# A hybrid decoder layer on one core: stores and parameter loads issued by GpSimd, the sampled tokens' loads by ScalarE

## The chip, the cores and the metric

The kernel runs on one core of one Trainium2 chip. The metric is the time of one execution on the device, in microseconds (us). Five engines work on the core: TensorE (PE in the profile; its weight loads are the row PEld), VectorE (DVE), ScalarE (ACT), GpSimd (POOL) and SyncE (SP). SP computes nothing; it issues transfers. A transfer (DMA) is issued by an instruction in the queue of SP, ACT or POOL, and an instruction that has to wait holds up everything behind it in the same queue.

## The reference

One layer with two token mixers and an MLP, in float32. It runs over a prompt of 2048 tokens and over a second batch of 8 x 4 sampled tokens that continue from given states; both use the same weights. Cut to what matters:

```python
xn = rms_norm(x, norm_mix_pre)
qk, v_m, o_m, gates, q_a, k_a, v_a = split(xn @ w_in)      # 1024 -> 2312 columns
qk, conv_new = short_conv(qk, conv_buf, conv_w)            # causal, 4 taps, silu
state_new, h = mlstm_chunk(state, (q, k, v, ig, lf))       # 4 heads, chunks of 128, state 64 x 128 per head
att = swa(q_a, k_a, v_a, sinks)                            # 8 heads, window 128, ALiBi, sinks
mix = concat(mlstm_output(h, o_m), rms_norm(att)) @ w_out
x = x + rms_norm(mix)
f = square(relu(rms_norm(x) @ w_up)) @ w_down              # 1024 -> 4096 -> 1024
x = x + rms_norm(f)
x = x + sigmoid(x @ w_pgate) * (p @ w_pproj)
```

It returns the new x of both batches and the new states: for each batch the mLSTM matrix C, its vector n and scalar m, the last three rows of the convolution's input, and the window's keys and values. For the sampled tokens C is 8 x 4 x 64 x 128.

## The kernel before

**Precision by pairs.** A matmul in float32 is done as three matmuls of a faster type: each operand is split into a high part, cast by ACT (L248 for weights, L227 for activations), and the rest, subtracted by DVE or POOL (L249, L228). For weights the helper is `wsplit` (L247), and `weng` (L242) gives the subtraction to POOL and DVE in turn.

**The ring of weights.** `Ring` (L251) holds 5 raw buffers and 7 pair buffers. A weight is asked for in the order of a plan written out by hand (L383). `get` (L270) loads it raw, splits it and, if the plan needs the same weight again, `keep` (L266) stores the finished pair, 512 KB, to DRAM; every later use reloads that pair (L274) instead of splitting again. A store in `keep` has to wait for the subtraction of its pair; a reload has to wait until TensorE has finished with the buffer that it overwrites. There are 242 such stores and 698 reloads.

**Stages.** First the projection by w_in over six chunks of the prompt, with attention (`swa_chunk`) and mLSTM (`mlstm_chunk`) running between its matmuls; their outputs go to DRAM as `yd` (L915, L1041). The sampled tokens' projection goes to DRAM as `zsd` (L591). Then three groups of blocks, each with w_out (`mix_mm`, `post_mix`, which stores x1 at L1429), sixteen steps of the MLP (`mlp`), and the gate (`gate_mm`, whose `finish` stores the output at L1765). From the fifth step of the first group (third of the later ones) the up matmuls use a product scheme with seven products for eight, whose weight sums are formed by `product` (L284), on POOL for the most part. A step of that kind splits and stores 7 pairs of w_up and 4 of w_down in the first group; the later groups reload nearly all.

**The sampled tokens.** In the first group's first steps `decode_mlstm` and `decode_swa` (L1070, L1256) run between the MLP's matmuls. They load states, caches and `zsd`; L1211 and L1212 load the mLSTM state into the tile `scs` in sixteen transfers, L1253 and L1254 store it in sixteen, half of them 128 KB and half 1 KB. The 1 KB ones (the vector n) write single numbers that lie apart in SBUF.

**Order.** TensorE's order is the program's, written out by the class `Flow`, which advances side work by estimated due times. The instructions of the other engines and queues are put in order at build time by a planner that takes what it reckons to be ready first. So the order of two instructions in a queue need not be the program's, and it is fixed when the kernel runs.

**Who issues.** All transfers of the program are issued by SP, with the exception of six small ones by ACT (L847). In the code, the name `dma` stands for SP's issue:

```python
    dma = nc.sync.dma_start
```

Of the kernel before, what the change touches and what calls it, by code (L numbers as in the profile page):

```python
# [24 lines left out]
DT = 4  # L25
# [170 lines left out]
def hybrid_layer(ctx: ExitStack, tc: tile.TileContext, A, O):  # L196
# [4 lines left out]
    dma = nc.sync.dma_start  # L201
# [49 lines left out]
    class Ring:  # L251
# [227 lines left out]
    def parameters():  # L479
        dma(prow[0:8], A["norm_ffn_pre"].rearrange("l (k p) -> (l k) p", p=P))  # L480
        dma(prow[8:12], A["mlstm_norm"].rearrange("l (k p) -> (l k) p", p=P))
        for s in range(2):
            dma(prow[12:16, s * AD : (s + 1) * AD], A["attn_norm"][:, s * 256 : (s + 1) * 256].rearrange("l (j d) -> (l j) d", d=AD))
        dma(prow[16:32], A["conv_w"].rearrange("l j (k p) -> (l j k) p", p=P))
        dma(bi[:, 0:1], A["b_gates"][:, 0:MH].rearrange("l h -> h l"))
        dma(bi[:, 1:2], A["b_gates"][:, MH : 2 * MH].rearrange("l h -> h l"))
        dma(sink, A["attn_sinks"][0:1, :].broadcast_to((P, AH)))
# [405 lines left out]
    def mlstm_chunk(r, blocks):  # L893
# [16 lines left out]
        def finish():  # L910
            if todo and len(r.get("o", ())) == len(blocks):
# [3 lines left out]
                dma(yd[blocks[i]][0], y)  # L915
# [64 lines left out]
    def swa_chunk(r, blocks):  # L980
# [45 lines left out]
        def values(i, j):  # L1026
# [14 lines left out]
            dma(yd[b][1], y)  # L1041
# [28 lines left out]
    def decode_mlstm(sp):  # L1070
        cb = sp.tile([P, NCB], F32, name="cb")
        dma(cb, A["const_b"][:, 0:NCB])
# [6 lines left out]
        dma(zqk, zsd[:, Z_QK : Z_QK + 512])  # L1079
        zg = sp.tile([NS, 2 * MH], F32, name="zg")  # L1080
        dma(zg, zsd[:, Z_G : Z_G + 2 * MH])


        for b in range(DB):
            dma(O[11][0, b], zsd[b * DT + 1 : b * DT + 4, Z_QK : Z_QK + 512])
        for out, cache, off in ((12, "cache_swa_k", Z_KA), (13, "cache_swa_v", Z_VA)):
# [3 lines left out]
            dma(oc[:, WIN - DT : WIN, :], zsd[:, off : off + 128].rearrange("(b t) c -> b t c", t=DT))  # L1090
# [87 lines left out]
        dma(va[:, :, 0:128], zsd[:, Z_V : Z_V + 512].rearrange("p (h v) -> p h v", h=MH))  # L1178
# [46 lines left out]
        dma(so, zsd[:, Z_O : Z_O + 512])  # L1225
# [4 lines left out]
        dma(yds[0], y)  # L1230
# [699 lines left out]
```

## Time and profile before

| | |
|---|---|
| Time, median of 3 runs | 2704.3 us (2697.03 to 2705.15) |
| The profiled execution | 2707.11 us, span 2705.3 us |
| TensorE's mean granted clock | 0.973 of full speed |
| Busy share of the span | PE 95%, PEld 82%, DVE 53%, ACT 36%, POOL 15% |
| Transfers | 626.95 MB, nearly all through SP's queue (q1) |
| HBM | 470.22 MB read, 155.25 MB written |

The span runs from the first instruction to the last of one execution. Busy shares do not count the issuing of transfers, so SP has none, and a queue that waits looks idle. In a row of the timeline the brackets say how long the engine stood still before the instruction and what ended that wait. In the chain of waits each piece is the work that the next piece waited for.

### The profile page before, as it was taken

How to read it: one execution, taken by the hardware profiler on the slowest of the kernel's cores; microseconds unless marked ns; L12 is line 12 of the kernel's file. 1: busy time of each engine (PE TensorE's matmuls, PEld its weight loads, DVE VectorE, ACT ScalarE, POOL GpSimd, SP SyncE). 2: the span in 40 equal slices, each digit the busy share in tenths (PEclk: the TensorE clock that was granted, in tenths of full speed). 3: DMA queues.
4: the chain of work that ended last, by engine and by line, in shares of the span. 5: the costliest groups of instructions: out<-in, count | busy, mean ns of one | idle time of the engine just before them, and what ended most of it. 6: DMA issues, size and time to landing. Idle time of an engine off the chain costs nothing.

```text
span 2705.3 us, 38958 instructions
## 1 busy us (share of the span) xinstructions
PE 2562.3 (95%) x14282; PEld 2227.0 (82%) x14282; DVE 1439.4 (53%) x3109; ACT 980.7 (36%) x2163; POOL 410.6 (15%) x517
## 2 busy tenths in 40 slices
PE   6899999999896899999999999999999998999998
PEld 5787888788675789888877888899988877999986
DVE  3675756655553275555573474444446345444453
ACT  3554454444443344433451352122223133222231
POOL 1310110100210134444440112000001010000010
PEclk8999999999898999999999999999999998999999
DMA  6766656567877547776688965555556885777786
GB/s 210 278 239 203 207 187 207 196 235 238 219 268 156 167 153 275 261 254 237 226 284 311 328 222 185 187 194 188 189 184 234 297 303 192 257 257 259 255 297 231
DMA packets 233728, 626.95 MB, mean 232 GB/s; under 512 B 37067, under 2 KB 76063, under 8 KB 233522
## 3 DMA queue, kind: packets, MB, share of 16 engines
q1 hardware_dynamic: 233490, 624.44, 68.0%
q8 instruction: 113, 1.85, 0.3%
q14 instruction: 77, 0.63, 0.1%
q10 hardware_dynamic: 48, 0.03, 0.0%
HBM read 470.22 MB, written 155.25 MB: 231 GB/s over the span
## 4 chain that ended last, share of the span: by engine, by line
PE 78%; DMA 8%; DVE 8%; ACT 2%; POOL 2%; issue 2%; SPq 1%; POOLq 0%; ACTq 0%; DVEq 0%
PE up L145 23%; PE dn L145 21%; PE mo L145 5%; PE pg L145 5%; PE v L145 3%; PE o L145 3%; DMA w<-wk 2%; PE gv L145 2%; PE qa L145 2%; PE pv L145 1%; PE aT L149 1%; PE aO L145 1%; PE qk L145 1%; DMA out_dram<-scs 1%; PE aS L145 1%
## 5 line engine op out<-in xcount | busy, mean ns | idle before, releaser
L145 PE MATMUL dn<-w,hh 128*128 128x512 f32 x1792 | 567.8, 398 | 15.4 <-DMA w<-wk 9.6
L145 PEld LDWEIGHTS dn<-w,hh 128*128 128x128 f32 x1792 | 334.3, 189 | 95.1 <-issue 11.3
L1683 DVE TENSOR_TENSOR f<-f,dn 128x512 f32<-128x512 f32 x420 | 287.7, 686 | 227.3 <-PE dn L145 226.5
L145 PE MATMUL dn<-w,hl 128*128 128x512 f32 x896 | 354.3, 395 | 0.0
L1647 DVE TENSOR_TENSOR re<-up,re 128x384 f32<-128x384 f32 (+1 forms) x280 | 144.3, 515 | 311.6 <-PE up L145 307.4
L145 PEld LDWEIGHTS dn<-w,hl 128*128 128x128 f32 x896 | 169.3, 189 | 39.4
L1648 ACT COPY re<-up 128x384 f32<-128x384 f32 (+1 forms) x40 | 17.9, 448 | 381.4 <-PE up L145 381.4
L249 POOL TENSOR_TENSOR w<-wr,w 128x512 fp32r<-128x512 f32 (+1 forms) x76 | 105.4, 1389 | 303.2 <-ACT w L248 199.7
L1573 ACT ACTIVATE re<-re 128x384 f32<-128x384 f32 (+1 forms) x160 | 78.8, 493 | 175.1 <-DVE re L1647 173.0
L248 ACT CAST w<-wr 128x512 fp32r<-128x512 f32 (+1 forms) x152 | 93.4, 619 | 132.0 <-DMA wr<-in_w_up_dram 29.5
L228 DVE TENSOR_TENSOR hl<-re,hh 128x384 fp32r<-128x384 f32 (+1 forms) x192 | 118.8, 619 | 38.1 <-ACT hh L227 37.6
L248 ACT CAST w<-wb 128x512 fp32r<-128x512 f32 x98 | 60.4, 621 | 199.7 <-PE dn L145 134.4
L145 PE MATMUL up<-ut00h,w 128*128 128x384 f32 x320 | 88.7, 348 | 24.7 <-ACT w L248 23.5
L249 DVE TENSOR_TENSOR w<-wr,w 128x512 fp32r<-128x512 f32 (+1 forms) x76 | 59.0, 778 | 83.1 <-ACT w L248 81.1
L249 POOL TENSOR_TENSOR w<-wb,w 128x512 fp32r<-128x512 f32 x70 | 93.8, 1359 | 54.1 <-ACT w L248 54.1
L1574 ACT ACTIVATE re<-re 128x384 f32<-128x384 f32 (+1 forms) x192 | 94.8, 494 | 5.9
L227 ACT CAST hh<-re 128x384 fp32r<-128x384 f32 (+1 forms) x192 | 92.5, 482 | 6.8
L1002 DVE CUSTOM_DVE_ANT_0 s<-aS,cst,sink 128x256 f32<-128x256 f32 (+1 forms) x128 | 56.9, 472 | 71.5 <-PE aS L145 71.2
L145 PE MATMUL up<-ut01h,w 128*128 128x384 f32 x320 | 88.9, 340 | 0.0
L1008 ACT ACTIVATE s<-s,swt 128x257 f32<-128x257 f32 (+1 forms) x128 | 63.4, 497 | 69.8 <-DVE swt L1005 69.0
L1394 POOL TENSOR_TENSOR f<-f,gffn 128x512 f32<-128x512 f32 x16 | 21.4, 1352 | 416.9 <-ACT j L1392 416.6
L145 PEld LDWEIGHTS up<-ut00h,w 128*128 128x128 f32 x320 | 60.2, 194 | 27.1 <-ACT w L248 24.3
(1468 smaller groups left out, 6305.4 us busy)
## 6 DMA issues: line engine op xcount, KB each, us to landing
w<-wk SPq DMA_DIRECT2D x678, 512.0 KB
wk<-w SPq DMA_DIRECT2D x238, 512.0 KB
wr<-in_w_down_dram SPq DMA_DIRECT2D x64, 256.0 KB
wb<-in_w_up_dram SPq DMA_DIRECT2D x28, 512.0 KB
w<-wk SPq DMA_DIRECT2D x20, 528.0 KB
x<-in_x_prompt_dram SPq DMA_DIRECT2D x16, 512.0 KB
y<-yd SPq DMA_DIRECT2D x32, 256.0 KB
xr<-in_x_prompt_dram SPq DMA_DIRECT2D x16, 512.0 KB
```

The costliest lines, as they stand in the source:

```text
L145: ins = self.pe.matmul(out, lhsT, rhs, start=start, stop=stop)
L149: self.issue(self.pe.transpose(out, src, ident), out, src, 2)
L227: act.copy(hi, src)
L228: dve.tensor_tensor(lo, src, hi.bitcast(F32), ALU.subtract)
L248: act.copy(hi, src)
L249: (eng or weng()).tensor_tensor(lo, src, hi.bitcast(F32), ALU.subtract)
L1002: dve.tensor_tensor_reduce(s_[:, s, lo : 2 * P], pS[:, s, lo:], bias[:, j, lo:], 1.0 if s == 0 else 0.0625, sink[:, h : h + 1], ALU.add, A ...
L1008: act.activation(e_, e_, AF.Exp, bias=nm[:, s : s + 1], accum_out=sm[:, s : s + 1])
L1573: act.activation(t, src, AF.Relu)
L1574: act.square(t, t)
L1647: add = lambda out, a, b: dve.tensor_tensor(out, a, b, ALU.add)
L1683: dve.tensor_tensor(out(i), out(i), ps[i], ALU.add)
```

## The change

Two further names are added. `put` issues on POOL's queue, `fetch_small` on ACT's. All stores except the two big copies from DRAM to DRAM (L1089) become `put`, and with them the eight loads of parameters; the loads in `decode_mlstm` and `decode_swa` become `fetch_small`. SP keeps the loads of x, weights, kept pairs, gains, y, Wt and p. Nothing else changes: the same transfers with the same shapes.

```diff
-    dma = nc.sync.dma_start
+    dma, put, fetch_small = nc.sync.dma_start, nc.gpsimd.dma_start, nc.scalar.dma_start
...
         def keep(self, key, t):
             self.kept[key] = dram.tile(list(t.shape), U32, name=f"{self.nm}k{len(self.kept)}")
-            dma(self.kept[key], t.bitcast(U32))
+            put(self.kept[key], t.bitcast(U32))
...
     def parameters():
-        dma(prow[0:8], A["norm_ffn_pre"].rearrange("l (k p) -> (l k) p", p=P))
+        put(prow[0:8], A["norm_ffn_pre"].rearrange("l (k p) -> (l k) p", p=P))
...
-        dma(zsd[:, zoff : zoff + n], t[:, :n])
+        put(zsd[:, zoff : zoff + n], t[:, :n])
...
-                dma(yd[blocks[i]][0], y)
+                put(yd[blocks[i]][0], y)
...
-                dma(cs[er, :, h, 0:128], c_in[e, h])
-                dma(cs[er, :, h, 128], n_in[e, h])
+                fetch_small(cs[er, :, h, 0:128], c_in[e, h])
+                fetch_small(cs[er, :, h, 128], n_in[e, h])
...
-                dma(c_out[e, h], cs[er, :, h, 0:128])
-                dma(n_out[e, h], cs[er, :, h, 128])
+                put(c_out[e, h], cs[er, :, h, 0:128])
+                put(n_out[e, h], cs[er, :, h, 128])
...
-        dma(bias_s, A["const_b"][:, NCB : NCB + nk])
+        fetch_small(bias_s, A["const_b"][:, NCB : NCB + nk])
...
-        dma(x1dst, f[b][:n])
+        put(x1dst, f[b][:n])
...
-        dma(O[2].rearrange("l b (p e) d v -> e d (l b p) v", e=2)[e], C[er, :, 0:128])
-        dma(O[3].rearrange("l b (p e) d -> e d (l b p)", e=2)[e], C[er, :, 128])
+        put(O[2].rearrange("l b (p e) d v -> e d (l b p) v", e=2)[e], C[er, :, 0:128])
+        put(O[3].rearrange("l b (p e) d -> e d (l b p)", e=2)[e], C[er, :, 128])
...
-        dma(dst, o[:n])
+        put(dst, o[:n])
```

## Rows read from the trace of the kernel before

**Rows 1.** The page, part 1: busy us (share of the span) and instructions.
```profile
PE 2562.3 (95%) x14282; PEld 2227.0 (82%) x14282; DVE 1439.4 (53%) x3109; ACT 980.7 (36%) x2163; POOL 410.6 (15%) x517
```
**Rows 2.** Windows: length, then busy us and count per engine, clock, DMA share, GB/s.
```profile
core 0: us, PE busy (x) PEld busy (x) DVE busy (x) ACT busy (x) POOL busy (x), PEclk, DMA share, GB/s
0.00:60.00 60.00, 36.74 (x171) 31.27 (x171) 23.84 (x46) 22.57 (x38) 10.96 (x23) 0.85 0.66 195
...
700.00:735.00 35.00, 26.33 (x96) 19.46 (x96) 21.52 (x37) 14.08 (x27) 5.17 (x5) 0.79 0.91 183
...
800.00:867.00 67.00, 57.77 (x307) 46.88 (x306) 34.17 (x90) 28.66 (x63) 7.37 (x8) 0.90 0.75 197
867.00:890.00 23.00, 1.76 (x7) 0.92 (x6) 0.84 (x1) 1.28 (x3) 1.27 (x1) 0.60 0.92 102
...
1038.00:1351.00 313.00, 313.00 (x1559) 281.42 (x1558) 177.38 (x270) 130.31 (x241) 144.08 (x109) 1.00 0.68 249
```
**Rows 3.** TensorE's timeline: start, us, instruction, in brackets its idle time before.
```profile
17.55 0.39 PE L145 MATMUL gv<-w,x0h 128*128 128x264 f32 x1 [2.40 <-ACT w L248]
...
22.21 1.11 PE L149 MATMUL x10t<-ident,x 128*128 128x128 f32 x4 [2.60 <-DVE x L584]
...
60.97 0.69 PE L145 MATMUL qa<-x0h,w 128*128 128x384 f32 x1 [4.87 <-ACT w L248]
...
733.58 1.22 PE L145 MATMUL mo<-w,yt00h 128*128 128x512 f32 x2 [5.34 <-DVE f L1488]
...
888.43 0.69 PE L145 MATMUL up<-ut00h,w 128*128 128x384 f32 x1 [20.85 <-ACT w L248]
```
**Rows 4.** SP's queue: what it waited for, us in total, times, longest.
```profile
SPq L268 <- POOL w L249: 363.0, 132, 11.0
...
SPq L268 <- DVE w L249: 99.0, 76, 7.6
```
**Rows 5.** The chain that ended last, 840 to 890: start, us, what.
```profile
856.73 20.28 DMA out_dram<-scs
...
877.66 0.60 SPq L359
...
878.31 10.17 DMA wr<-in_w_up_dram
```
**Rows 6.** POOL's timeline, at the start and from 845 to 890.
```profile
5.95 0.57 POOL L499 TENSOR_TENSOR x0t<-x0t,nhalf 128x1 f32<-128x1 f32 x1 [4.82 <-DVE x0t L498]
...
850.51 1.28 POOL L249 TENSOR_TENSOR w<-wr,w 128x512 fp32r<-128x512 f32 x1 [4.49 <-ACT w L248]
888.51 1.27 POOL L249 TENSOR_TENSOR w<-wr,w 128x512 fp32r<-128x512 f32 x1 [36.72 <-DMA wr<-in_w_up_dram]
```
**Rows 7.** The chain that ended last, 700 to 735.
```profile
706.58 9.32 DMA out_dram<-C
...
715.91 13.77 DMA wr<-in_w_out_dram
```
**Rows 8.** SP's timeline at the start: start, us, instructions that follow one another.
```profile
9.82 2.05 SPq L268 DMA_DIRECT2D wk<-w  x3
...
12.96 1.78 SPq L456 DMA_DIRECT2D x<-in_x_prompt_dram  x2
```
**Rows 9.** Issues by line, ns min/median/max, first and last start; L268 from 1038 to 1351.
```profile
L268 SPq DMA_DIRECT2D wk<-w x110: 319/320/929, 1039.7 to 1349.2; - x110
...
L847 ACTq DMA_DIRECT2D mbd<-Mt x6: 246/246/514, 57.4 to 617.1; - x6
...
L1211 SPq DMA_DIRECT2D scs<-in_state_mlstm_c_dram x8: 602/615/705, 820.7 to 835.3; - x8
```
**Rows 10.** TensorE's waits for reloaded pairs: us in total, times, longest.
```profile
PE dn L145 <- DMA w<-wk: 9.6, 3, 4.8
...
PE mo L145 <- DMA w<-wk: 7.3, 3, 3.8
```
**Rows 11.** SP's timeline at the end.
```profile
2702.64 0.33 SPq L1765 DMA_DIRECT2D out_dram<-ots  x1
```

More of the change, by code (lines that the diff above doesn't have):

```diff
@@ L479, in parameters @@
     def parameters():
-        dma(prow[0:8], A["norm_ffn_pre"].rearrange("l (k p) -> (l k) p", p=P))
-        dma(prow[8:12], A["mlstm_norm"].rearrange("l (k p) -> (l k) p", p=P))
+        put(prow[0:8], A["norm_ffn_pre"].rearrange("l (k p) -> (l k) p", p=P))
+        put(prow[8:12], A["mlstm_norm"].rearrange("l (k p) -> (l k) p", p=P))
         for s in range(2):
[L483 to L487, printed above, removed]
+            put(prow[12:16, s * AD : (s + 1) * AD], A["attn_norm"][:, s * 256 : (s + 1) * 256].rearrange("l (j d) -> (l j) d", d=AD))
+        put(prow[16:32], A["conv_w"].rearrange("l j (k p) -> (l j k) p", p=P))
+        put(bi[:, 0:1], A["b_gates"][:, 0:MH].rearrange("l h -> h l"))
+        put(bi[:, 1:2], A["b_gates"][:, MH : 2 * MH].rearrange("l h -> h l"))
+        put(sink, A["attn_sinks"][0:1, :].broadcast_to((P, AH)))
         yield 5.0
@@ L1040, in values @@
             act.copy(y.rearrange("p (j q) -> p j q", j=4), pO)
-            dma(yd[b][1], y)
+            put(yd[b][1], y)
             sq = sw.tile([P, 512], F32, tag="ya", name=f"sq{b}")
@@ L1071, in decode_mlstm @@
         cb = sp.tile([P, NCB], F32, name="cb")
-        dma(cb, A["const_b"][:, 0:NCB])
+        fetch_small(cb, A["const_b"][:, 0:NCB])
         mask_s = cb[:, 0:32]
@@ L1078, in decode_mlstm @@
         zqk = sp.tile([NS, 512], F32, name="zqk")
-        dma(zqk, zsd[:, Z_QK : Z_QK + 512])
+        fetch_small(zqk, zsd[:, Z_QK : Z_QK + 512])
         zg = sp.tile([NS, 2 * MH], F32, name="zg")
-        dma(zg, zsd[:, Z_G : Z_G + 2 * MH])
+        fetch_small(zg, zsd[:, Z_G : Z_G + 2 * MH])
         for b in range(DB):
-            dma(O[11][0, b], zsd[b * DT + 1 : b * DT + 4, Z_QK : Z_QK + 512])
+            put(O[11][0, b], zsd[b * DT + 1 : b * DT + 4, Z_QK : Z_QK + 512])
         for out, cache, off in ((12, "cache_swa_k", Z_KA), (13, "cache_swa_v", Z_VA)):
@@ L1224, in decode_mlstm @@
         so = sp.tile([NS, 512], F32, name="sso")
-        dma(so, zsd[:, Z_O : Z_O + 512])
+        fetch_small(so, zsd[:, Z_O : Z_O + 512])
         act.activation(so, so, AF.Tanh, scale=0.5)
@@ L1229, in decode_mlstm @@
         mlstm_finish(num, col[:, 8:12], so, y, NS, "dm")
-        dma(yds[0], y)
+        put(yds[0], y)
         for h in range(MH):
@@ L1266, in decode_swa @@
         vc = sp.tile([WIN, DB, 128], F32, name="svc")
-        dma(kc, A["cache_swa_k"].rearrange("l b s k d -> s (l b) (k d)"))
-        dma(vc, A["cache_swa_v"].rearrange("l b s k d -> s (l b) (k d)"))
+        fetch_small(kc, A["cache_swa_k"].rearrange("l b s k d -> s (l b) (k d)"))
+        fetch_small(vc, A["cache_swa_v"].rearrange("l b s k d -> s (l b) (k d)"))
         snk = sp.tile([P, 2], F32, name="ssnk")
@@ L1271, in decode_swa @@
         for g in range(4):
-            dma(snk[g * NS : (g + 1) * NS], sv[:, :, g].broadcast_to((NS, 2)))
+            fetch_small(snk[g * NS : (g + 1) * NS], sv[:, :, g].broadcast_to((NS, 2)))
         yield 15.0
@@ L1338, in decode_swa @@
         dve.tensor_scalar(y, y, rs[:NS], None, ALU.mult)
-        dma(yds[1], y)
+        put(yds[1], y)
     def decode():
@@ L1351, in hybrid_layer @@
     for o, c0 in ((6, 8), (7, 136)):
-        dma(O[o].rearrange("l b s k d -> (l b s) (k d)"), prev["va"][:, c0 : c0 + 128])
+        put(O[o].rearrange("l b s k d -> (l b s) (k d)"), prev["va"][:, c0 : c0 + 128])
     es_proj.close()
@@ L1532, in hybrid_layer @@
     dve.tensor_copy(cvo, pcv[:3, :])
-    dma(O[5].rearrange("l b j c -> (l b j) c"), cvo)
+    put(O[5].rearrange("l b j c -> (l b j) c"), cvo)
     es1.close()
```

16 lines of the change are left out of this document (8 added, 8 removed).

## The prediction

> **What bounds the kernel now.** Read the page's busy line first: TensorE's matmuls are busy 2562.3 of 2705.3 us [rows 1], so whatever the change does to other engines can only shorten the 143 us in which TensorE stands still, or lengthen them. The table by stage says where those lie [rows 2]: 23.3 us of 60 at the start (60 less 36.74), 8.7 of 35 between the projection and the first MLP, 21.2 of 23 in 867 to 890, and none of 313 in the ten steps from 1038 to 1351. Then TensorE's own timeline, for what ended each pause [rows 3]: one pause of 20.85 us waits for ACT's cast of a raw row of w_up; the others are of 2 to 5 us. Last the queue that issues the transfers: SP spent 363.0 us waiting for GpSimd's residual and 99.0 us for DVE's, both times only to be able to store a weight pair (L268) [rows 4]. In most of that time TensorE had work, so those sums are not the gain; what matters is what stood behind such a store in a stage where TensorE was dry.
>
> **The moved stores, one place at a time.** 377 issues leave SP for POOL: 242 weight pairs, 34 of y, 32 of yd, 17 of x1, 16 of the sampled state and 36 small ones. Their bytes stay the same; what changes is who stands behind them.
>
> *867 to 890.* The chain there is a store of scs that lands after 20.28 us, then at 877.66 the issue of the load of w_up (L359), which lands 10.17 us later [rows 5]. The split of the pair that it feeds starts on POOL at 888.51; the one before it ran at 850.51 and was over at 851.8 [rows 6]. From then on a raw buffer was free, so without the sixteen stores of scs ahead of it the load could go some 25 us earlier, at about 853, while TensorE first needs it at 867.6 (888.43 less 20.85). That leaves 14 us for a load that took 10.2 among the stores, plus cast 0.6 and split 1.3. But the same sixteen stores now stand in POOL's queue, and the odd split is POOL's: it may wait behind them. Bounds: nothing gained, or all 20.85. I take 16, nearer the upper end, because the data of the last store is there at 858 and only its slow landing holds the others.
>
> Against this stands a rule of the Trainium skill (DMA: Bandwidth & Descriptors, "Issuing engines are not separate DMA queues"): transfers issued by SP, ACT and GpSimd run on the same 16 engines and interleave, so another issuer saves issue time only. The row agrees that engines and not only the queue are short there: 0.92 busy at 102 GB/s [rows 2]. By the rule the early load would still share those engines with the stores; I make that a rival below.
>
> *700 to 735.* The same picture, smaller: two stores of C land after 9.32 us, a load of w_out behind them after 13.77 [rows 7], and TensorE pauses 5.34 at 733.58 [rows 3]. I take 4 (0 to 5.3).
>
> *Start.* SP issues three pair stores at 9.82, each waiting for its split, and only then at 12.96 the loads of x1 and x2 [rows 8]. TensorE pauses 2.40, 2.60 and 4.87 in the first 61 us behind such loads [rows 3]; I take 5 of these 9.9. Against it the eight parameter loads come to POOL, which at 5.95 must compute the first rstd (L499) [rows 6]; if they go ahead of it they cost 2 us at 0.25 each, the issue price on ACT [rows 9], or up to 5. I take 2. Net 3 gained.
>
> *Later loads.* Waits of TensorE for reloaded pairs sum to 9.6 (dn) and 7.3 (mo) [rows 10]. Most end when a buffer of the ring comes free, which the change does not touch, so I take 3 of 16.9 (0 to 10).
>
> **What POOL pays.** No row shows a DMA issued by POOL, so its price must be bounded. From below: 0.25 us, the issue on ACT, or 0.32, the same store on SP [rows 9]. From above there is no row, so I ask what POOL can bear. In the ten steps 1038 to 1351 it is busy 144.1 of 313 us and 110 pair stores fall there: (313 - 144.1) / 110 = 1.54 us of free time for each [rows 2, 9]. Up to that, less some for waits, the stores hide in POOL's idle time, and TensorE, at 100% there, does not feel them. I take 0.3 to 1.2 as likely, nearest to the SP row, and cost the steps at nothing; if that cover is gone each 0.1 us above 1.54 costs 12 x 11 x 0.1 = 13 us over the twelve steps. In between, a store in POOL's queue waits for DVE or ACT with POOL's next work behind it: sink copies (L998), the powers (L1406, L887), half of the pair splits. On SP these waits were 99 us for DVE's splits alone [rows 4]. Nearly all lie where TensorE is fed ahead; I take 3 us lost (0 to 10).
>
> The Trainium skill prices a GpSimd issue higher (DMA: Bandwidth & Descriptors, "Specifications"): about 1 us to the first byte against 0.6 for SP and ACT, descriptors being written by GpSimd itself. An estimate from that page: 14.4 + 11 x 1.0 = 25.4 us of POOL per step of 31.3, which still fits. No run here shows it yet.
>
> **What ACT pays.** 32 loads of the sampled tokens come to ACT between 735 and 895: at 0.25 us, ACT's row, 8 us; at 0.615, SP's row for the sixteen loads of scs, 20 us [rows 9]. ACT is busy 28.7 of 67 us there [rows 2], so over half falls in gaps, but relu and casts queue behind each block. I take 4 lost (0 to 10). SP loses the same issues; that is already in the 16 above.
>
> **End.** The last store goes out at 2702.64, after DVE's last operation, and the span ends at 2705.3 [rows 11]; issued by POOL it may land later by the unknown issue price: 1 lost (0 to 2).
>
> **Sum:** -16 - 4 - 3 - 3 + 3 + 4 + 1 = -18. The profiled execution took 2707.1 us (span 2705.3), 2.8 above the median of 2704.3; so 2707.1 - 18 = 2689 on its scale, and **2686** on the median's.
>
> **Rivals.**
> *POOL becomes the bound (slower).* If a pair store holds POOL for more than 1.54 us in the twelve steps, TensorE runs dry there. At 1.9 us that is 12 x 11 x 0.36 = 48 lost: 2686 + 48 = 2734. For it: POOL's splits share their stretch with DVE's, and waits for DVE come on top. Against: ACT's and SP's issues are 0.25 to 0.6. Chance 0.20. The Trainium skill (SBUF — State Buffer, "Who interferes with whom") speaks for this one: a DMA issued by GpSimd waits for its descriptors while some DVE modes hold a shared port; no row here shows such a wait.
> *The engines, not the queue (no change).* The early loads of 867 to 890 and 700 to 735 crawl beside the slow stores, so 16 becomes 4 and 4 becomes 0: -18 + 16 = -2, 2702. For it: engines 0.92 busy there. Against: the load had the stores ahead of it in its own queue when it took 10.17 us. Chance 0.20.
> *The stall changes its owner.* The split on POOL waits behind the sixteen stores until about 888, and ACT's 32 issues cost 10 instead of 4: -18 + 16 + 6 = +4, 2708. Chance 0.12; that the move is in the program's text but the order on the engines ends up the same is within it.
> *My forecast* keeps 0.48, with its own range 2666 to 2700.
>
> **Chances.** A measurement of this kernel can tell about 0.3%, 8 us. Faster: 0.48 of the forecast less a little, plus the better part of the second rival: 0.52. Within: 0.25. Slower: 0.23, the first rival and the end of the third. The range reaches from 2660 (the upper bounds of 700 to 735, the start and the late loads all met) to 2738 (the first rival).
>
> **What would show it.** The pause of 20.85 before an up matmul near 888 shrinks to about 5 and L359's load is issued near 853; x1's load is issued by 8 us; POOL's rows in the steps stay under 31 us with the issues counted, and TensorE stays at 100% there. It is wrong if TensorE pauses for POOL L249 in the steps (first rival), if the same pause stays and ends on DMA wr<-in_w_up_dram (second) or on POOL L249 (third), or if pauses appear behind ACT's issues.

## The result and the profile after

The changed kernel takes 2687.6 us (median of 5 runs, 2683.6 to 2687.7), the kernel before 2700.5 (5 runs, 2697.0 to 2705.2): ratio 0.9945, 95% interval 0.9931 to 0.996. The forecast was 2686. The profiled execution took 2687.7 us, with a span of 2685.6 against 2705.3 [rows 1]. So the two traces differ by 19.7 us, the medians by 12.9: the profiled execution of the kernel before was 6.6 us over its median. What follows accounts for the 19.7.

First the busy line of the page (engine, busy us, share, instructions):

```profile
PE 2546.3 (95%) x14282; PEld 2216.1 (83%) x14282; DVE 1473.3 (55%) x3109; ACT 981.4 (37%) x2163; POOL 613.3 (23%) x894
```

GpSimd's row now counts its 377 issues as instructions (894, and 517 before) and as busy time.

TensorE's idle time is 2685.6 - 2546.3 = 139.3 us, and was 2705.3 - 2562.3 = 143.0: only 3.7 us less. The other 16.0 us are TensorE's busy time itself, for the same instructions. The mean granted clock rose from 0.973 to 0.980: (1 - 0.973) x 2705.3 / 0.5 = about 146 us at the lower of its two levels (1.2 GHz) before, (1 - 0.980) x 2685.6 / 0.5 = about 107 us after. So the sum of idle time says little here, and neither do equal windows of time. To see where the time went, cut both traces at the same matmul (TensorE runs the same matmuls in the same order in both). The windows of the changed kernel so cut (columns: stretch and length, then as in [rows 2]: busy us and instructions of PE, PEld, DVE, ACT and POOL, granted clock, busy share of the DMA engines, GB/s):

```profile
0.00:51.20 51.20, 31.93 (x178) 29.80 (x179) 20.07 (x30) 20.31 (x36) 23.28 (x45) 0.93 0.90 278
51.20:98.90 47.70, 36.81 (x191) 33.28 (x189) 41.73 (x95) 25.89 (x60) 22.97 (x33) 0.86 0.80 273
...
691.10:748.90 57.80, 53.49 (x229) 41.34 (x230) 36.31 (x67) 26.04 (x50) 20.65 (x29) 0.93 0.91 276
748.90:805.40 56.50, 36.49 (x166) 29.87 (x164) 26.16 (x66) 18.83 (x40) 15.33 (x18) 0.82 0.70 232
805.40:874.60 69.20, 60.32 (x329) 50.62 (x328) 27.51 (x74) 24.19 (x53) 22.71 (x33) 0.93 0.77 162
...
1000.70:1365.50 364.80, 356.83 (x1758) 316.63 (x1757) 225.82 (x308) 151.17 (x279) 228.33 (x249) 1.00 0.64 244
...
2170.20:2280.10 109.90, 99.85 (x562) 85.25 (x561) 61.18 (x120) 43.79 (x96) 15.28 (x23) 0.95 0.74 266
```

Beside them the same work in the kernel before, from the same view of its trace (us):

```
work from .. to (before)   length before -> after   change   idle before -> after   clock
0 .. 63.1                    63.1 ->  51.2          -11.9       24.2 -> 19.3        0.84 -> 0.93
63.1 .. 101.7                38.5 ->  47.8           +9.3        2.9 -> 10.9        0.96 -> 0.86
101.7 .. 141.9               40.2 ->  34.6           -5.6        4.1 ->  1.2        0.92 -> 1.00
141.9 .. 641.3              499.5 -> 496.3           -3.2       19.2 -> 17.9        1.00 -> 1.00
641.3 .. 700.3               58.9 ->  61.2           +2.3        4.0 ->  6.5        0.95 -> 0.92
700.3 .. 770.2               70.0 ->  57.8          -12.2       11.3 ->  4.3        0.85 -> 0.93
770.2 .. 808.5               38.3 ->  56.5          +18.2        3.4 -> 20.0        0.96 -> 0.82
808.5 .. 901.3               92.8 ->  69.3          -23.5       30.5 ->  8.9        0.83 -> 0.93
901.3 .. 1021.6             120.2 -> 126.1           +5.9        1.4 ->  5.8        1.00 -> 0.99
1021.6 .. 1375.5 (steps)    354.0 -> 364.7          +10.7        0.0 ->  8.0        1.00 -> 1.00
1375.5 .. 2180.8            805.3 -> 804.7           -0.6       14.4 -> 12.0        0.99 -> 0.99
2180.8 .. 2300.8            120.0 -> 109.9          -10.1       15.8 -> 10.1        0.90 -> 0.95
2300.8 .. 2705.3            404.5 -> 405.5           +1.0       11.9 -> 14.6        0.99 -> 0.99
```

The net of -19.7 is 67 us gained less 47 given back. The 9.3 given back at 63.1 to 101.7 is a pause of 10.72 us (second line of the next block). DVE's recorded order now has L903, which stands until the transfer Wt<-mbd has landed (issued 65.48, 7.63 us), ahead of the tile s that TensorE waits for, and TensorE comes there 14 us earlier (63.91 for 78.18). No run takes it apart. TensorE's timeline names what ended the pauses that remain (start, length, [idle before <- releaser]); these answer to [rows 3]:

```profile
14.36 1.11 PE L149 MATMUL x00t<-ident,x 128*128 128x128 f32 x4 [14.36 <-DVE x1t L498]
...
74.63 0.66 PE L149 MATMUL aT<-ident,s 128*128 128x128 f32 x2 [10.72 <-DVE s L1012]
...
769.99 1.22 PE L145 MATMUL mo<-w,yt01h 128*128 128x512 f32 x2 [13.40 <-DMA w<-wk]
...
787.38 1.22 PE L145 MATMUL mo<-w,yt01h 128*128 128x512 f32 x2 [6.60 <-ACT f L1486]
...
854.87 0.69 PE L145 MATMUL up<-ut00h,w 128*128 128x384 f32 x1 [5.02 <-ACT f L1681]
...
879.93 0.69 PE L145 MATMUL up<-ut01h,w 128*128 128x384 f32 x1 [4.83 <-ACT re L1573]
...
1137.56 0.73 PE L145 MATMUL dn<-w,hh 128*128 128x512 f32 x2 [1.74 <-DVE f L1683]
```

The pause of 20.85 us is gone; three of 3 to 5 us stand in its place, one of them (862.88, 3.39 us, POOL w L249) not shown. They are at other matmuls: the one that waited 20.85 us now waits for nothing (858.87). New are 13.40 and 6.60 in the output projection, and ten waits of up to 1.7 us (8.0 in all) for DVE's sum L1683 in the steps.

**770 to 808.** The waits of SP's queue, then of ACT, between 735 and 800 (us in total, times, longest):

```profile
SPq L274 <- DMA scs<-in_state_mlstm_n_dram: 26.9, 3, 23.3
```
```profile
ACT sso L1226 <- DMA w<-wk: 17.0, 1, 17.0
```

(The second row names a transfer on the same semaphore; what L1226 reads is so, whose load ACT issued at 767.45.)

SP, whose queue now has only loads, stood 23.3 us (742.0 to 765.3) ahead of a reload of a weight pair until a load of scs had landed that ACT issued. The reload neither reads nor writes scs. In the record of this stretch SP's queue stands 23.31 us at a wait for two semaphores that ACT's transfers update. The transfers of SP and ACT take turns on the same eight, and one that is to use a semaphore first waits for the transfer that had it last. GpSimd's transfers there use eight others. Two queues so become one where the program's order interleaves them.

**The steps.** DVE's groups with the first line of the step's work, and GpSimd's store (count | busy us, mean ns | idle before), from the windows 1010 to 1375:

```profile
L1683 DVE TENSOR_TENSOR f<-f,dn 128x512 f32<-128x512 f32 x136 | 91.5, 684 | 65.6 <-PE dn L145 65.6
...
L249 DVE TENSOR_TENSOR w<-wr,w 128x512 fp32r<-128x512 f32 x23 | 30.4, 1324 | 1.8
...
L249 DVE TENSOR_TENSOR w<-wb,w 128x512 fp32r<-128x512 f32 x20 | 26.6, 1331 | 0.9
...
L268 POOL DMA_DIRECT2D wk<-w x121 | 66.7, 552 | 20.4 <-DVE w L249 10.9 <-POOL w L249 7.7 <-DVE re L1647 1.3
```

A store holds GpSimd 0.55 us, but DVE's splits take 1.32 us where they took 0.71 and 0.68 before. Not all of them do: in the steps as cut above 24 of 43 take 0.69, and 18, some two a step, 1.98 to 2.47. One of these, with GpSimd beside it (start, length):

```profile
1054.80 1.10 POOL L268 DMA_DIRECT2D wk<-w  x2
...
1055.73 2.04 DVE L249 TENSOR_TENSOR w<-wr,w 128x512 fp32r<-128x512 f32 x1
...
1055.92 1.30 POOL L249 TENSOR_TENSOR w<-wr,w 128x512 fp32r<-128x512 f32 x1
```

DVE's split starts during GpSimd's issue, GpSimd's own split follows the issue at once, and DVE's ends 0.55 us after GpSimd's. Where DVE's split starts as little ahead of an instruction of GpSimd with no issue running, it keeps its 0.69, and GpSimd's is the longer one (1.70 for 1.30):

```profile
1289.37 0.69 DVE L249 TENSOR_TENSOR w<-wb,w 128x512 fp32r<-128x512 f32 x1
1289.52 1.70 POOL L298 TENSOR_TENSOR wb<-wb,wb 128x512 f32<-128x512 f32 x1 [2.22 <-DMA wb<-in_w_up_dram]
```

Eight splits in this trace started during an issue with nothing of GpSimd right behind; they took 0.69 too. After a long split the sums L1683 come late, and TensorE waits for them.

### The profile page after: what moved, and what is told of

It reads as the page before. It is cut to its first block, busy times and chain, and to the rows that moved or that the text cites. A ratio compares the mean times of both kernels' runs of the same rounds, so it can differ in the third digit from the quotient of the medians.

```text
span 2685.6 us, 39181 instructions
## 1 busy us (share of the span) xinstructions
PE 2546.3 (95%) x14282; PEld 2216.1 (83%) x14282; DVE 1473.3 (55%) x3109; ACT 981.4 (37%) x2163; POOL 613.3 (23%) x894
## 4 chain that ended last, share of the span: by engine, by line
PE 72%; DMA 9%; DVE 8%; issue 4%; POOL 3%; ACT 3%; ACTq 0%; SPq 0%; POOLq 0%; DVEq 0%
PE up L145 19%; PE dn L145 19%; PE pg L145 6%; PE mo L145 4%; PE v L145 3%; PE o L145 2%; PE qk L145 2%; DMA wk<-w 2%; PE gv L145 2%; POOL w L249 2%; PE pv L145 1%; PE aT L149 1%; PE aO L145 1%; DMA w<-wk 1%; PE qa L145 1%
## 5 line engine op out<-in xcount | busy, mean ns | idle before, releaser
L1683 DVE TENSOR_TENSOR f<-f,dn 128x512 f32<-128x512 f32 x420 | 285.7, 686 | 218.0 <-PE dn L145 217.7
L268 POOL DMA_DIRECT2D wk<-w x242 | 134.1, 555 | 145.6 <-DVE w L249 109.6
L249 POOL TENSOR_TENSOR w<-wr,w 128x512 fp32r<-128x512 f32 (+1 forms) x76 | 102.0, 1342 | 81.8 <-ACT w L248 62.8
L249 POOL TENSOR_TENSOR w<-wb,w 128x512 fp32r<-128x512 f32 x70 | 89.9, 1295 | 100.8 <-ACT w L248 100.3
L249 DVE TENSOR_TENSOR w<-wr,w 128x512 fp32r<-128x512 f32 (+1 forms) x76 | 80.5, 1061 | 44.4 <-ACT w L248 42.4
```

The costliest lines, as they stand in the source:

```text
L249: (eng or weng()).tensor_tensor(lo, src, hi.bitcast(F32), ALU.subtract)
L268: put(self.kept[key], t.bitcast(U32))
L1683: dve.tensor_tensor(out(i), out(i), ps[i], ALU.add)
```

## The experiments

Each ratio is of 4 to 12 runs against 11 to 23 of the kernel before on the same chip. The change of each stretch against the kernel before, cut at the same matmuls, from the profiled execution of each (us):

```
                    0   142   641   700   770   808   901  steps  1376  2181  2301
                 -142  -641  -700  -770  -808  -901 -1022        -2181 -2301  -end    sum
changed          -8.2  -3.2  +2.3 -12.2 +18.2 -23.5  +5.9  +10.7  -0.6 -10.1  +1.0  -19.7
e1_small_on_sync -10.3 -4.2  +2.3 -10.1  -5.5 -21.1  +4.8  +10.9  -4.5 -10.5  -0.2  -48.4
e2_pairs_on_sync -7.2  -1.4   0.0  -7.9 +18.2  -6.6  +0.1    0.0  -3.6 -10.8  -2.6  -21.8
e3_only_pairs   -14.7  -0.9 +10.4 -10.7  -5.6  -2.7  +0.4  +14.9  -2.8  -0.6  -1.3  -13.6
e4_outputs_only  +0.2  -5.6  +0.2  -7.0  -1.5 -10.4  +0.4    0.0  -3.7 -10.9  -3.2  -41.5
e5_first68      -16.8  +0.1  +2.1 -11.7  -5.5 -18.8  +6.6    0.0  -3.3 -10.7  +3.6  -54.4
e6_only_small    -1.4  +0.5  +0.2  -0.8  +6.7 -19.3  +4.9    0.0  -3.4  +0.8  -1.1  -12.9
e7_own_stores   -12.2  -2.5  +1.4  -9.6  -5.5 -13.9  +4.8  +11.9  -6.6  -9.5  +1.4  -40.3
e8_issue_no_wait +15.0 +12.9  0.0  -8.9  -0.3 -11.7  +6.4    0.0  -3.8 -11.4  +1.3   -0.5
e9_hold         -16.6  -2.5  +2.2 -12.3  -5.6 -18.8  +3.1   +0.7  -3.2 -10.2  +3.0  -60.2
e10_tail        -16.6  -3.0  +2.9 -13.7  -5.5 -19.5 +10.6    0.0  -3.2 -12.3  -3.8  -64.1
e11_small_on_pool -12.2 -2.7 +2.7 -12.0 +18.3 -24.4  +0.6  +11.2  -5.2 -10.5  +5.7  -28.5
e12_o_first     -11.8  -4.0  +2.3 -11.8 +14.1 -24.2  +7.0  +11.0  -0.6 -10.3  +1.5  -26.8
```

Each row is one execution against one. The sums lie 5 to 13 us lower than the ratios say, because the profiled execution of the kernel before was a long one; so a few us in a single column carry no argument, and effects are read from columns that differ by more. Medians of different runs come from different chips and are compared by their ratios. The first four runs move single parts.

**e1_small_on_sync** (changed kernel):

```diff
-    dma, put, fetch_small = nc.sync.dma_start, nc.gpsimd.dma_start, nc.scalar.dma_start
+    dma, put, fetch_small = nc.sync.dma_start, nc.gpsimd.dma_start, nc.sync.dma_start
```

> The changed kernel with the 32 loads of the sampled tokens back on SyncE. Theory (coupled queues): in the changed kernel SP stood 23.3 us at a reload of a weight pair (L274) until loads of scs that ACT had issued had landed, and TensorE then paused 13.4 us; ACT, not free for evacuations, added 6.6. With the loads on SP that wait has no cause: the stretch from the second MLP block's transposes (748 to 805 in the changed kernel, 57 us; 38.7 in the kernel before) goes back to 39 to 43 us, and of the 18 us up to 10 are given back just after, since SP again issues the sixteen scs loads at 0.61 us each. Time 2670 to 2680. Rival (transfers): the reloads are late because the engines carry the scs loads, the cache copies and the x1 stores at the same time, whoever issues them; then the pause stays at over 8 us and the time at 2683 to 2692.

2661.1 us, ratio 0.987 (0.9852 to 0.9888): some 20 us under the changed kernel by the ratios (0.9945 less 0.987), 26.5 by the medians, and faster than forecast. The stretch 770 to 808 takes 38.3 - 5.5 = 32.8 us, and of its 23.7 us only 2.4 are given back at 808 to 901, less than I allowed. The rival falls: the same transfers, issued by SP, cost nothing there. SP issues them 19 us later (771.9 for 752.9), but the engines are not idler for it: from 735 to 770 they are busy 0.90 of the time here without a pause, 0.70 in the changed kernel with it.

**e2_pairs_on_sync** (changed kernel):

```diff
-            put(self.kept[key], t.bitcast(U32))
+            dma(self.kept[key], t.bitcast(U32))
```

> The changed kernel with the 242 stores of weight pairs back on SyncE. Theory (DVE meets POOL): in the ten-odd steps the changed kernel needs 10.7 us more, because two DVE splits a step last 2.0 to 2.4 us instead of 0.69 where they meet a store and a split of POOL; without the stores on POOL the splits in the steps last 0.7 on average and the steps have 354 us again, not 365. The start loses its gain of 8 us, and the pauses behind pair stores at 640 to 735 come back in part (up to 10); the pause of 20 us near 880 does not come back, since it was the sixteen scs stores. Time 2680 to 2698. Rival (POOL's own time): the steps are slower because POOL is held 0.56 us for each issue; it expects the same for the steps, but the mean of DVE's splits in the steps stays above 1.0. Rival (pairs make the gain): the pause near 880 comes back with over 12 us and the time is 2700 or more.

2685.9 us, ratio 0.996 (0.9947 to 0.9974). The steps have their 354.0 us again and DVE's splits their 0.69, as the theory said. But a pause of over 20 us near 880, which it excluded, is there:

```profile
889.07 0.69 PE L145 MATMUL up<-ut01h,w 128*128 128x384 f32 x1 [21.39 <-ACT f L1681]
```

It is not the old one: it stands at a later matmul, and what TensorE waits for there is another load. A load of w_down, issued right behind a pair store that had waited for its split (853.52), was in flight for 26.50 us beside the scs stores that GpSimd had issued (839.1 to 861.4); the median of such a load is 5.9. ACT's cast waits for it, then ACT's own loads hold it a further 6.54 us.

```profile
853.89 26.50 DMA wr<-in_w_down_dram
```

In these 26.5 us the DMA engines are all busy (1.02) at 141 GB/s.

**e3_only_pairs** (kernel before):

```diff
-            dma(self.kept[key], t.bitcast(U32))
+            nc.gpsimd.dma_start(self.kept[key], t.bitcast(U32))
```

> The kernel before with only the 242 stores of weight pairs moved to GpSimd. Theory: the loss in the steps is there whole (+8 to +12, DVE's splits there at 1.2 to 1.4 us on average), the start gains 5 to 8, the stretch 748 to 805 loses nothing (no load on ACT), and the pause near 888 stays at over 8 us, because the sixteen scs stores still stand ahead of the load of w_up on SP. Time 2688 to 2704. Rival (pairs make the gain): the pause near 888 goes, and the time is 2670 to 2685.

2696.1 us, ratio 0.9998 (0.9988 to 1.0007): no change, as expected, because what the start and 700 to 770 gain goes in the steps (+14.9, where 8 to 12 were expected) and at 641 to 700. A stall of 17.72 us stands at an earlier matmul:

```profile
856.60 0.69 PE L145 MATMUL up<-ut00h,w 128*128 128x384 f32 x1 [17.72 <-ACT f L1681]
```

Here too a load of w_down is what ACT's cast waits for: issued at 829.93 among the scs stores, landed at 855.34.

**e4_outputs_only** (changed kernel with pairs, parameters and small loads on SyncE):

```diff
-    dma, put, fetch_small = nc.sync.dma_start, nc.gpsimd.dma_start, nc.scalar.dma_start
+    dma, put, fetch_small = nc.sync.dma_start, nc.gpsimd.dma_start, nc.sync.dma_start
-            put(self.kept[key], t.bitcast(U32))
+            dma(self.kept[key], t.bitcast(U32))
     def parameters():
-        put(prow[0:8], A["norm_ffn_pre"].rearrange("l (k p) -> (l k) p", p=P))
+        dma(prow[0:8], A["norm_ffn_pre"].rearrange("l (k p) -> (l k) p", p=P))
...
```

> The kernel before with only the stores of outputs and of activations (y, yd, x1, C, scs and the small ones) on GpSimd; pair stores, parameter loads and the loads of the sampled tokens on SyncE. Theory: the pause near 888 shrinks from 20.85 to under 8, the steps keep their 354 us, the start keeps its 63, nothing is lost at 748 to 805: 2700.5 - 15 to - 24, so 2677 to 2686. Rival (pairs make the gain): the time stays at 2695 to 2703, since SP still waits for splits before it can load.

2665.6 us, ratio 0.9893 (0.9877 to 0.9909), faster than forecast, but not for the reason given: a pause of 13.72 us remains, again behind a load of w_down (issued 842.79, landed 869.03),

```profile
870.26 0.69 PE L145 MATMUL up<-ut01h,w 128*128 128x384 f32 x1 [13.72 <-ACT f L1681]
```

and 10.9 us come at 2181 to 2301, which gains only in the runs that have the outputs' stores on GpSimd (e3 and e6 have not: -0.6 and +0.8). In the kernel before a reload stands there behind a store of x1 (issued at 2243.50, when DVE has its data; the reload at 2243.87, and TensorE has waited 3.12 at 2248.96); on GpSimd that store holds no reload.

**e5_first68** (e1 with the parameters on SyncE, and):

```diff
-            put(self.kept[key], t.bitcast(U32))
+            (put if len(self.kept) <= 68 else dma)(self.kept[key], t.bitcast(U32))
```

> Only the first 68 pair stores (those before about 895 us) and the stores of outputs and activations on GpSimd; the other 174 pair stores, the parameter loads and the loads of the sampled tokens on SyncE. If each stage keeps what the four single runs showed: against the run with the small loads on SyncE (2661.1) the steps give back 10.9 us, the stretch after 901 gives back 5, and the start, with the parameters on SyncE, 4: 2641, range 2632 to 2650. Rival (the steps lose for another reason than the pair stores on GpSimd, or the start's gain needs the parameters on GpSimd): 2652 to 2664.

2654.5 us, ratio 0.9837 (0.9815 to 0.9859): better than both kernels, but 4 us above the range and in the rival's, whose reason fails all the same: the steps came to 354.0 and the start, with the parameters on SyncE, gained more than forecast (-16.8); the stretch from 901 did not recover (+6.6), and the end took 3.6 us more.

**e6_only_small** (kernel before, the 32 loads on ScalarE):

```diff
-        dma(cb, A["const_b"][:, 0:NCB])
+        fetch_small(cb, A["const_b"][:, 0:NCB])
...
```

> The kernel before with only the 32 loads of the sampled tokens moved to ScalarE. Theory (coupled queues): SP stands some 20 us at a reload until ACT's loads of scs have landed, TensorE pauses over 8 us on w<-wk between 740 and 800, and the time is 2712 to 2726. Rival (ACT's issues hide and the pause of the changed kernel comes from the traffic that its other moves brought forward): no wait of SP on a load of scs over 5 us, time 2692 to 2704.

2695.2 us, ratio 0.9994 (0.9979 to 1.0009). My figure fell: at least 12 us were to be lost. The waits of SP at 735 to 800 are there, but short,

```profile
SPq L274 <- DMA scs<-in_state_mlstm_n_dram: 7.4, 1, 7.4
...
SPq L274 <- DMA zqk<-zsd: 5.5, 1, 5.5
```

and cost 6.7 us; against that 808 to 901 gains 19.3, probably because SP no longer issues the sixteen scs loads at 0.61 us there [rows 9]: the loads of w_down and w_up were out by 835.1, ahead of the scs stores (845.1 to 872.2). So that stretch shortens with any of the three moves (outputs, small loads, less so pairs), and they don't add up: once the other two are made, the small loads on ACT give 2.4 us there (e1) and cost 23.7 before it.

**e7_own_stores** (e1, and):

```diff
-            put(self.kept[key], t.bitcast(U32))
+            (put if eng is pool else dma)(self.kept[key], t.bitcast(U32))
...
```

(`eng` is the engine that split the pair, handed down in the lines left out.)

> The run with the small loads on SyncE, with one thing more: pairs that DVE split are stored by SyncE, so that GpSimd stores only the pairs that it split itself and never waits for DVE to store one. Theory (order): what lengthens the splits on DVE in the steps is that GpSimd, held at a store until DVE's split before is done, starts its own next split just when DVE starts one; without the wait the mean of DVE's splits there is under 0.9 us, the steps need 354 to 358 us, and the time is 2648 to 2656. Rival (the issue itself: GpSimd's issuing holds DVE, or takes its time): half of the issues stay, the mean stays at 1.0 or more, the steps need 359 us or more, time 2657 to 2664.

2667.5 us, ratio 0.9883 (0.9862 to 0.9904), steps +11.9, over both forecasts. The theory falls: GpSimd waits for no split of DVE here (80 stores instead of 121 in the steps), and DVE's splits are as long (1.27 on average):

```profile
1071.42 1.09 POOL L270 DMA_DIRECT2D wk<-w  x2
...
1072.42 1.97 DVE L251 TENSOR_TENSOR w<-wr,w 128x512 fp32r<-128x512 f32 x1
...
1072.52 1.31 POOL L251 TENSOR_TENSOR w<-wr,w 128x512 fp32r<-128x512 f32 x1
```

(L270 and L251 are L268 and L249 of the other kernels.)

**e8_issue_no_wait** (e4, and):

```diff
             dma(self.kept[key], t.bitcast(U32))
+            d = dram.tile([P, 32], U32, name=f"{self.nm}d{len(self.kept)}")
+            put(d, ident[:, 0:32].bitcast(U32))
```

> The run with only the outputs' stores on GpSimd (2665.6), with one thing more: for every pair GpSimd issues a further transfer, of 128 bytes a partition from a constant to a scratch tile that nothing reads, which waits for no split. Theory (order): GpSimd's 242 issues without a wait leave the steps at 354 us and DVE's splits there at 0.7 to 0.8 us; time 2660 to 2671. Rival (the issue itself): the steps need 358 us or more with DVE's splits at 1.0 or more; time 2672 to 2685.

2706.7 us, ratio 1.0032 (1.0016 to 1.0047). It does not test what it was made for: waiting for nothing, the 242 transfers were all ordered into the first 200 us (GpSimd's group there):

```profile
L270 POOL DMA_DIRECT2D wd<-ident x242 | 130.3, 545 | 21.8 <-DMA wd<-ident 13.7 <-DMA ident<-in_const_a_dram 3.7 <-issue 3.7
```

What it does show is GpSimd as the bound: busy 169.2 of 200 us, and 0 to 641 is 27.9 us longer than before, 33 longer than in e4.

**e9_hold** (e5, and, for pairs that GpSimd split):

```diff
+            if len(self.kept) > 68 and eng is pool:
+                for _ in range(2):
+                    tc.keep_in_program_order(pool.memset(hold, 0.0))
...
```

(`hold` is a tile of 128 x 352.)

> The run with the first 68 pair stores on GpSimd (2654.5), with one thing more: behind each of its later splits whose pair is stored (by SyncE, as in that run) GpSimd writes zeros twice into a scratch tile of 128 x 352 that nothing reads. No transfer is issued by GpSimd there; it only comes later to its next split, by an estimated 0.6 to 0.8 us a pair (its 128x16 memset took 0.14 us, its 128x1 0.10). Theory (time): the stores cost the steps 10.9 us because the 0.56 us of each push GpSimd's next splits to where DVE splits, and two instructions that read SBUF on both engines run one after the other; then the steps need 359 to 366 us here as well, with splits of 1.9 to 2.4 us on DVE, and the time is 2659 to 2668. Rival (the issue: writing a transfer's descriptors is what holds DVE): no descriptors are written in the steps, so they keep 354 to 356 us with DVE's splits at 0.7 to 0.8, time 2650 to 2657.

2648.5 us, ratio 0.9815 (0.9794 to 0.9837). Steps +0.7 us, where e7, with as many stores in the place of the memsets, had +11.9. Two memsets take 0.85 us; an issue with the 0.30 us wait ahead of it 0.86. So the time that GpSimd is held makes at most a small part of the loss; the rival holds, except that the time is 1.5 us below its range and DVE's splits are a little over its 0.8 (0.94 and 0.81): 30 of 43 take under 0.8, the others 1.0 to 1.6. How they meet here:

```profile
L251 DVE TENSOR_TENSOR w<-wr,w 128x512 fp32r<-128x512 f32 x23 | 21.6, 939 | 2.3 <-ACT w L249 0.5
...
L251 DVE TENSOR_TENSOR w<-wb,w 128x512 fp32r<-128x512 f32 x21 | 17.0, 808 | 1.0
...
L273 POOL MEMSET hold<- 128x352 f32 x158 | 62.1, 393 | 5.2
```
```profile
1059.45 0.83 POOL L273 MEMSET hold<- 128x352 f32 x2
...
1060.13 0.69 DVE L251 TENSOR_TENSOR w<-wr,w 128x512 fp32r<-128x512 f32 x1
...
1060.24 1.73 POOL L251 TENSOR_TENSOR w<-wr,w 128x512 fp32r<-128x512 f32 x1
```

DVE's split starts 0.11 us ahead of GpSimd's, runs its 0.69, and GpSimd's is the longer one (1.73). In the rows of the changed kernel and of e7 DVE's starts 0.10 and 0.19 us ahead and is the one held, with an issue instead of memsets before.

**e10_tail** (e5, and):

```diff
-        put(dst, o[:n])
+        (dma if b == "s" or b >= NB - 2 else put)(dst, o[:n])
```

> The run with the first 68 pair stores on GpSimd (2654.5), with the last outputs (the last two blocks of the prompt and the sampled rows) stored by SyncE. In the kernel before the span ends 2.7 us after the last store is issued by SP, in that run 7.7 us after GpSimd issues it. Theory: the last landing is what the span waits for, so 3 to 5 us go: 2649 to 2652. Rival (the end is longer because of the clock, not the queue): 2653 to 2656.

2643.4 us, ratio 0.9794 (0.9772 to 0.9816), the best of all: 11 us under e5, where 3 to 5 were expected. The end accounts for 7.4 of it (+3.6 to -3.8). The last store in e5 and in e10:

```profile
2643.24 0.51 POOL L1765 DMA_DIRECT2D out_dram<-ots  x1 [2.13 <-DVE ots L1763]
```
```profile
2638.53 0.33 SPq L1765 DMA_DIRECT2D out_dram<-ots  x1
```

The spans end at 2650.9 and 2641.2: 7.7 and 2.7 us later, as the theory has it. Its reason fails: the last store has landed 1.9 us after its issue in e5 and 1.6 in e10. What ends last in e5 is GpSimd's closing drain (6.90 us, from 2643.22; 0.09 in e10), for which the other engines wait. The same row in the changed kernel (ns min/median/max):

```profile
L1926 POOLq DRAIN  x3: 46/102/5261, 2679.6 to 2685.4; - x3
```

The rest of the 11 us is not accounted for.

**e11_small_on_pool** (changed kernel):

```diff
-    dma, put, fetch_small = nc.sync.dma_start, nc.gpsimd.dma_start, nc.scalar.dma_start
+    dma, put, fetch_small = nc.sync.dma_start, nc.gpsimd.dma_start, nc.gpsimd.dma_start
```

> The changed kernel with the 32 loads of the sampled tokens on GpSimd instead of ScalarE. Theory (coupled queues): SP's reload waits for scs loads only because SP and ACT hand on the same semaphores; GpSimd's transfers use others, so SP's wait at 742 is under 3 us and the pause of 13.4 us goes. GpSimd pays 32 x 0.6 = 19 us between 735 and 860, most of it in idle time; time 2658 to 2674. Rival (the loads come ahead of the reloads and take the engines, whoever issues them): a pause on w<-wk of over 8 us stays between 740 and 800; time 2680 to 2695.

2678.3 us, ratio 0.9924 (0.9905 to 0.9943): between both forecasts, and a third cause. SP waits for no load of scs any more and the reloads are in time, but 770 to 808 is as long as in the changed kernel (+18.3):

```profile
784.79 1.22 PE L145 MATMUL mo<-w,yt01h 128*128 128x512 f32 x2 [21.20 <-ACT f L1486]
```
```profile
ACT sso L1226 <- DMA sso<-zsd: 20.3, 1, 20.3
```

ACT stands at the activation of so, the last of the row of small loads, and the evacuation that TensorE needs is behind it on ACT. In e1 that activation is ordered later, at 795.7, and waits 0.8 us.

**e12_o_first** (changed kernel; the activation L1226 keeps its place):

```diff
         fetch_small(zg, zsd[:, Z_G : Z_G + 2 * MH])
+        so = sp.tile([NS, 512], F32, name="sso")
+        fetch_small(so, zsd[:, Z_O : Z_O + 512])
...
-        so = sp.tile([NS, 512], F32, name="sso")
-        fetch_small(so, zsd[:, Z_O : Z_O + 512])
```

> The changed kernel with one load of the sampled tokens earlier: that of so (L1225), the last of the row, is issued ahead of the sixteen scs loads; the activation that reads it (L1226) keeps its place in ACT's order. In the changed kernel ACT stood 17.0 us at L1226, and 20.3 in the run with these loads on GpSimd, where TensorE paused 21.2 us for ACT's evacuation (L1486) though SP waited for no scs load. Theory A (two holds): SP's wait of 23.3 us for scs stays, since nothing of it changes; the pause on w<-wk stays at 10 to 14 us and only the 6.6 us behind ACT go; time 2678 to 2684. Theory B (ACT's hold makes all): with L1226 not waiting both pauses go, the stretch from 748 needs 39 to 44 us instead of 57, and the time is 2662 to 2672. If neither pause moves, both are wrong: 2685 to 2691.

2680.2 us, ratio 0.994 (0.9924 to 0.9957), which can't be told from the changed kernel's 0.9945. By the trace theory A holds: the wait for scs stays, the pause on w<-wk too, and what stood behind ACT halves.

```profile
764.60 1.22 PE L145 MATMUL mo<-w,yt01h 128*128 128x512 f32 x2 [11.85 <-DMA w<-wk]
...
779.36 0.73 PE L145 MATMUL mo<-w,yt01h 128*128 128x512 f32 x2 [3.20 <-ACT f L1486]
```
```profile
SPq L274 <- DMA scs<-in_state_mlstm_n_dram: 27.0, 3, 22.2
```

In the changed kernel the two holds lie one after the other, 13.4 and 6.6; take one away (e11) and the other fills the gap.

## Why the prediction was right, point by point

The time was right (2687.6 for 2686); the way to it was half right, and that the two agree so well is luck. The -18 were to come off a median of 2704.3, which two more runs put at 2700.5, so the medians differ by 12.9; the traces differ by 19.7. And the gains, 58 with the start taken as one, were more than twice the 26 of the sum, the losses 38 (+2.3 +18.2 +5.9 +10.7 +1.0) instead of 8: two errors of some 30 us that cancelled. Of the range, the low end does not follow from the three bounds named for it, which give about 2671, and the upper 2738 is 4 us over its rival's 2734 without a reason.

*867 to 890, -16.* Right in kind and near in size: L359's load is issued 22.6 us earlier, close to the 853 that I named (the row joins four loads),

```profile
855.08 14.33 SPq L359 DMA_DIRECT2D wr<-in_w_up_dram  x4
```

and TensorE's idle time from 805 to 875 is 21.6 us less than in the same work before. The stretch is 23.5 shorter, because the slow clock behind the pause goes too (0.83 to 0.93). What I had wrong is what comes next. The matmul that waited 20.85 us waits for nothing in any of the runs; what is left are pauses for loads that are in flight together with the scs stores, whoever issues these. In the changed kernel that load of w_up lands after 12.9 us (10.2 before), three of w_down after 13.6 to 19.8, and ACT waits for two of these:

```profile
853.71 0.62 ACT L248 CAST w<-wr 128x512 fp32r<-128x512 f32 x1 [6.91 <-DMA wr<-in_w_down_dram]
```

They were issued early enough (840.0 to 844.2) that TensorE loses 5.02 and 3.39 us. With outputs moved alone (e4), with pairs alone (e3) and with pairs left on SP (e2) a load of w_down took 25.4 to 26.5 us, and the pauses are 13.7, 17.7 and 21.4; pairs and outputs moved together (e1) give 21.1 of the 23.5.

*700 to 735, -4.* Undersized: -12.2 from 700 to 770 less 2.3 lost at 641 to 700. The pause of 5.34 is gone, idle time falls by 7.0, and the clock rises from 0.85 to 0.93.

*Start, -3.* -8.2 net. The three waiting stores went, as argued, and x1's load is issued at 6.5. The parameter loads were priced at the wrong place:

```profile
5.13 0.60 POOL L487 DMA_DIRECT2D sink<-in_attn_sinks_dram  x1
...
6.04 0.57 POOL L499 TENSOR_TENSOR x0t<-x0t,nhalf 128x1 f32<-128x1 f32 x1
...
10.91 2.20 DVE L249 TENSOR_TENSOR w<-wr,w 128x528 fp32r<-128x528 f32 x1 [1.14 <-ACT w L248]
...
13.03 1.27 DVE L584 SCALAR_TENSOR_TENSOR x<-x,x0t,gpre 128x1024 f32<-128x1024 f32 x1
```

All eight are issued before L499, yet it starts at 6.04, 0.1 us late [rows 6]. The 2 us fell elsewhere: the recorded order now puts L584 behind two splits on DVE, the second of them 2.20 us long beside an issue and a split of GpSimd as in the steps, and the first matmul starts at 14.4 instead of 8.2. With the parameters on SP it starts at 7.9 (e5) and 0 to 142 gains 16.8.

*Later reloads, -3.* Undersized: -10.1 at 2181 to 2301, which e4 puts down to the moved stores of x1 and outputs. In the kernel before, a reload stood behind such a store (the times under e4), where I took most of these waits for waits on a buffer.

*Pair stores on GpSimd, 0.* The term that failed. The price was inside my bounds (0.55 us, against 0.32 on SP [rows 9]), and well under the 1.54 us at which the first rival was to begin. Yet the steps lost 10.7. I asked whether GpSimd has the time, and it has; the cost came by DVE, whose splits are held where one meets an issue with GpSimd's split right behind. e2, e5 and e10 take the pair stores away and the loss with them; e7 and e9 show that neither GpSimd's waits for DVE nor, but for a small part, its time make it. What in the issue does it stays open. That the two engines hold each other could have been read before: in the same steps of the kernel before a DVE instruction with both inputs in SBUF takes 0.55 us or up to 1.43 (ns min/median/max):

```profile
L228 DVE TENSOR_TENSOR hl<-re,hh x46: 546/584/1431, 1022.2 to 1369.0; 128x384 fp32r<-128x384 f32 x46
```

The price that the Trainium skill gives (DMA: Bandwidth & Descriptors, "Specifications"), about 1 us to the first byte, is not what an issue holds GpSimd: the row L268 of the steps has 0.55. The Trainium skill (SBUF — State Buffer, "Who interferes with whom") says that a DVE instruction with two SBUF inputs contends with a GpSimd instruction that reads SBUF, that the shared ports are an exclusive lock, and that the order of issue decides who blocks. The trace agrees on who is concerned: the split with two SBUF inputs takes up to 2.47 us, the sum L1683 with one input in PSUM 0.67 to 0.69. It agrees on the order in e9 and where no issue runs (1289.37), not beside an issue, where the records have DVE first and held.

*ACT's issues, +4 (0 to 10).* Out of its bounds: in the changed kernel the loads on ACT cost some 20 us (e1, by the ratios). I counted what ACT spends on issuing. The cost was SP waiting on ACT's transfers, and ACT's own evacuations behind an activation whose load came last. The "pauses behind ACT's issues" that I named as a sign are there, 6.6 us, and 4.83 at 879.93, where ACT had stood 18.52 us: it was held at its own loads of the caches and sinks, one of which waited until the scs stores had landed, the next for a load of SP with the same semaphore.

*GpSimd's waits, +3; end, +1.* The first can't be told apart. The end is 3.3 us longer: the last store is issued 6.0 us before the span's end, 2.7 in the kernel before [rows 11]; I had allowed 2. It is not the landing, as I had it (1.87 us after the issue, 1.61 on SP), but GpSimd's closing drain of 5.26 us (e10).

```profile
2679.60 0.51 POOL L1765 DMA_DIRECT2D out_dram<-ots  x1 [2.13 <-DVE ots L1763]
```

*The rivals.* GpSimd did not become the bound in the steps (228.3 of 364.8 us busy). The engines did hold the early loads (12.9 to 19.8 us in flight with the engines busy 0.96 of the time at 143 GB/s, 840 to 863), so the second rival was right about the cause and wrong about the size: the loads went early enough to leave 8 us of pauses. 3.4 us of the stall went over to GpSimd's split.

*What the sum left out.* Its first premise was that the change can only shorten or lengthen TensorE's idle time, and every term was the length of a pause. Of the 19.7 us 16.0 are TensorE's busy time: the granted clock is lower in the stretch behind a long pause (0.82 over the stretch with the 13.4 and 6.6, 0.96 over the same work before). So a pause costs more than it is long (700 to 770: 7.0 us less idle, 12.2 shorter), and a new one too.

## What to carry to other kernels

Cut two traces at the same matmul before comparing: equal windows and sums of idle time hid 67 us gained and 47 lost. A stall that comes back near the same time need not be the same stall: look which matmul waits, and for which transfer. A queue that is freed of stores is not free if its transfers share semaphores with another queue's, and a load moved to an idle queue may bring its consumer ahead of more urgent work on an in-order engine. Move the stores that wait, where TensorE is dry, and leave them where it is fed (e10, with the first 68 pairs and all outputs but the last on GpSimd: 0.9794 of the time before).

## What the runs showed of the hardware that was not expected

- A DVE instruction of 0.69 us with both inputs in SBUF took 1.98 to 2.47 us in 18 cases in the steps where it started during an issue of GpSimd with a tensor instruction of GpSimd right behind. Beside an issue alone it took 0.69 (8 cases). With memsets as long in the place of the issue 30 of 43 took under 0.8 us, none over 1.6. What in the issue does this was not tried.
- The span ended 2.7 to 3.0 us after the last store where SP issued it, 3.5 to 10.4 us after where GpSimd did. The store itself landed after 1.6 and 1.9 us; GpSimd's closing drain took 2.8 to 9.6 us then, 0.1 where SP issued the last stores. What sets its length was not tried.
- SP's queue stood 22 to 23 us for transfers that ACT had issued, of tiles that it did not touch.
- Loads of 256 KB, 5.9 us in the median, took 25.4 to 26.5 us beside the sixteen scs stores in three runs, whether SP or GpSimd had issued these.
